# Blocks transposed as float32 in one instruction each, and a group's two sequences kept on the halves of the array

## The chip, the core and the metric

One core of a Trainium2 chip runs the whole program in one launch. The metric is the time of an execution on the device, in microseconds (us). The core has TensorE (PE in the profile; its weight loads are PEld), VectorE (DVE), ScalarE (ACT), GpSimd (POOL) and SyncE (SP), which issues the transfers here. TensorE writes to PSUM alone; the other engines copy from there.

## What is computed

Two layers of a decoder on 1024 tokens of width 1024, all float32. Layer A is gated linear attention with four heads. Layer B, which the change is mostly about, is attention of 8 query heads over three groups of shared keys and values. In group g a query attends keys at distances 0, d, 2d, ..., up to a window:

```python
SWA_GROUPS = ((128, 1), (512, 4), (2048, 16))     # (window, dilation d)
scores = jnp.einsum('brnqgpe,brnkge->brngpqk', qb, kcat)      # per subsequence t = i*d + r
scores = jnp.where(mask, scores, -jnp.inf)
m = jnp.max(scores, axis=-1, keepdims=True)
p = jnp.exp(scores - m)
den = jnp.sum(p, axis=-1)
o = jnp.einsum('brngpqk,brnkge->brnqgpe', p, vcat) / den
lse = m + jnp.log(den)
# over the groups:
wts = jax.nn.softmax(jnp.stack(lses, axis=0), axis=0)
o = jnp.sum(wts[..., None] * jnp.stack(outs, axis=0), axis=0)
y = (o * jax.nn.silu(g)) @ w_out
```

With 1024 tokens the third group (number 2 in the code, dilation 16) has sixteen subsequences of 64 tokens, and its window covers all earlier tokens of the same subsequence.

## The kernel before

The whole program is recorded first, as operations on named tiles; the class `Sched` then sorts them. Its `order()` (line 249) gives each engine its instructions by the earliest time at which they can start in a model of the chip; the durations come from `cost()` (line 521), among them 0.057 us for a two-byte transpose and a rate of 190 KB/us for transfers, to which line 352 adds 2.0 us until they land. Where an operation may run on several engines (`S.va` is VectorE or ScalarE, `S.vap` also GpSimd), the model picks one. The chip gets one fixed order per engine; so every change of a cost re-sorts the whole program. Nearly all instructions are issued from line 441, so the profile's groups are told apart by tile names.

A projection (`project`) multiplies weights by activations in three products of rounded parts (`wh` by `xh`, `wh` by `xl`, `wl` by `xh`; `x1h` and `x1l` in layer B), 512 columns each, into a PSUM tile `acc`. Weights come as 512 KB tiles `wf` and are split into `wh` and `wl` ahead of use.

Layer B has eight units, one per query head (`u`). `q_proj(u)` makes the three `Q`; `scores(u)` multiplies `Q` by the shared keys `K` into tiles `lv`, adds a mask and takes the row's minimum of the negated scores on VectorE (`P<-lv,bmask` or `rmask`), and takes the exponential on ScalarE. The row statistics `sts` go through DRAM (`std`, `nat`, `cwd`, `cw`), since the three groups order their queries differently, and come back as one weight per row. `attend(u)` scales `P` by these weights, transposes its blocks with `turn_blocks` (line 655) into `PT`, and multiplies by the values `V` into `po`. `turn_blocks` also turns layer A's keys (`ke` to `kh`, 8 blocks a head) and, in `rows`, half of the residual stream (`x1f` to `x1r`, 4 blocks for each of 8 tiles).

`turn_blocks` treats a float32 block as two planes of 16 bits, lying interleaved in memory. Each plane is transposed by itself as bfloat16 against `identb`, into a PSUM tile `ms` that keeps the planes apart, and two copies (of `uint16`) put them together again: per block two weight loads and two matmuls, per group of three or four blocks two copies.

Group 2 lies in eight blocks of 128 positions (`BL[2]`, line 1229). A block holds the tokens with the same remainder by 8, which are two subsequences of dilation 16; the 128x128 scores of the two against each other are masked by `rmask`, and their zeros are multiplied by `V` like the rest. A unit has 8, 12 and 15 blocks to turn in groups 2, 1 and 0.

In the profile a float32 product is two records on PE, each with its own weight load; a rounded one (`wh` by `xh`) or a two-byte transpose is one record.

Of the kernel before, what the change touches and what calls it, by code (L numbers as in the profile page):

```python
# [15 lines left out]
T = 1024  # L16
# [123 lines left out]
class Sched:  # L140
# [108 lines left out]
    def order(self):  # L249
# [62 lines left out]
        while n_done < len(ops):  # L312
# [37 lines left out]
            if e == "SP":  # L350
                dma_free = max(dma_free, st) + c
                o.t1 = dma_free + 2.0
                free[e] = st + 0.1
# [167 lines left out]
def cost(e, meth, n, outs, ins, args, kw):  # L521

    if e == "PE":
        if meth == "transpose":
            return 0.057 if ins[0].dtype == BF else 0.215
# [48 lines left out]
def trunk(tc, xT, wP, wA, wAv, wa, w2, b2, ng, wO, wK, wV, wB, wOB, lng, lnb,  # L574
# [80 lines left out]
    def turn_blocks(dst, blocks):  # L655


        n = len(blocks)
        pt = ps.tile([128, 2, 4, 128], BF, name="ms", bufs=2)
        with S.group():  # L660
            for i, b in enumerate(blocks):
                for s in range(2):
                    S.tensor.transpose(pt[:, s, i, :], b[:, s, :], identb)
        to = dst.halves(U16)
        pu = pt.bitcast(U16)
        for s in range(2):
            S.va.copy(to[:, s, :], pu[:, s, :n, :].rearrange("p a b -> p (a b)"))
# [10 lines left out]
    identb = const.tile([128, 128], BF, name="identb")  # L678
# [5 lines left out]
    def load_consts():  # L684
        S.sync.dma_start(ident, ident_d)
        S.vector.tensor_copy(identb, ident)
# [23 lines left out]
    def layer_a(t2, t1, after):  # L710
# [200 lines left out]
        def state_prep(h):  # L911
# [13 lines left out]
            for g in range(2):  # L925
                turn_blocks(kh[:, g * 512:g * 512 + 512],
                            [ke.halves(BF)[:, :, c * 128:c * 128 + 128] for c in range(4 * g, 4 * g + 4)])
# [181 lines left out]
    vd = [dram.tile([T, 256], F32, name=f"vd{i}") for i in range(2)]  # L1109
# [13 lines left out]
    def tok_view(ap, g):  # L1123
        if g == 2:
            return ap.rearrange("p (n a b) -> p n a b", n=4, a=16)
        return ap.rearrange("p (i r) -> p i r", r=DIL[g])

    def layer_b(xs):
        bmask = hp.tile([128, 256], F32, name="bmask", bufs=1)
        S.sync.dma_start(bmask, bmask_d)  # L1130
        rmask = hp.tile([128, 128], F32, name="rmask", bufs=1)
# [29 lines left out]
        def proj_v(g):  # L1161
            stage = {}

            def evac(j, acc):
# [8 lines left out]
                if g == 2:  # L1173

                    S.sync.dma_start(vd[1].rearrange("(a n b) e -> n a b e", a=16, n=8)[j], dst)
                elif j % 4 == 3:
                    h = j // 4 * 512
                    S.sync.dma_start(vd[g - 1][h:h + 512, :].rearrange("(n p) e -> p n e", p=128),
                                      pg.rearrange("p (n e) -> p n e", n=4))
# [381 lines left out]
```

## Time and profile before

| | us |
|---|---|
| median of 3 runs (lowest to highest) | 1208.53 (1208.48 to 1209.45) |
| the profiled execution | 1207.9 |
| its span, first to last instruction | 1206.1 |
| TensorE busy in it | 1185.7 |
| VectorE, ScalarE, GpSimd busy | 754.1, 529.9, 219.6 |

The span is what the trace covers; 1.8 us of the execution lie outside it. Busy times are unions of an engine's instructions. Matmuls overlap, so that a record's own length (219 ns for a two-byte transpose) is longer than the distance to the next one's start; the distance is what it takes of the engine.

### The profile page before, as it was taken

To read this page: it belongs to the slowest core of one execution; us is meant where nothing else is said; L and a number is where in the kernel's file an instruction comes from. 1 tells how busy PE (TensorE), PEld (TensorE's weight loads), DVE (VectorE), ACT (ScalarE), POOL (GpSimd) and SP (SyncE) were. 2 spreads that over 40 slices of the span, in tenths; PEclk is the share of its full clock that TensorE was granted. 3 is DMA by queue.
4 is the path that set the end of the run, shared out by engine and by line. 5 is a ranking of instruction groups with operands and counts; after the bars stand their busy time and mean duration, and the time that the engine had idled before them with its cause. 6 is when DMAs were issued, how large, how long until landed. Compare 5 with 4: busy or idle time off the path is not lost.

```text
span 1206.1 us, 20729 instructions
## 1 busy us (share of the span) xinstructions
PE 1185.7 (98%) x8340; PEld 1017.2 (84%) x8340; DVE 754.1 (63%) x1448; ACT 529.9 (44%) x1070; POOL 219.6 (18%) x145
## 2 busy tenths in 40 slices
PE   9999999999999999999999999999999999999996
PEld 7888978988988887789988888888888888888885
DVE  5482962943967698962255655564656566657468
ACT  5452534433563344422114554545362545456242
POOL 0011101211222122420031213040312130203200
PEclk9999999999999999999999999999999999999999
DMA  8102111111243462554411111111412020124545
GB/s 264 41 20 70 36 54 53 59 49 36 71 165 114 148 211 99 196 184 141 131 56 41 46 37 54 37 53 36 132 46 55 36 55 19 38 63 133 172 133 183
DMA packets 93648, 107.57 MB, mean 89 GB/s; under 512 B 43792, under 2 KB 63248, under 8 KB 93552
## 3 DMA queue, kind: packets, MB, share of 16 engines
q1 hardware_dynamic: 93552, 106.25, 28.3%
q8 instruction: 65, 1.06, 0.4%
q14 instruction: 31, 0.25, 0.1%
HBM read 85.06 MB, written 21.17 MB: 88 GB/s over the span
## 4 chain that ended last, share of the span: by engine, by line
PE 88%; DVE 8%; issue 2%; ACT 1%; DMA 1%; POOL 0%; SPq 0%; DVEq 0%; ACTq 0%; POOLq 0%
PE acc L441 62%; PE po L441 9%; PE lv L441 9%; PE ms L441 4%; PE pro L441 3%; DVE rt L441 2%; DVE X L441 2%; DVE wl L441 1%; DVE oT L441 1%; DVE x1l L441 1%; DMA xf<-in_xT 1%; ACT wh L441 0%; DMA cosT<-in_cos 0%; DVE t L441 0%; DVE sq L441 0%
## 5 line engine op out<-in xcount | busy, mean ns | idle before, releaser
L441 PE MATMUL acc<-x1h,wh 128*128 128x512 f32 x608 | 252.2, 415 | 2.0 <-DVE t L441 1.5
L441 PE MATMUL acc<-x1l,wh 128*128 128x512 f32 x608 | 237.5, 391 | 0.7 <-DVE x1l L441 0.6
L441 PE MATMUL acc<-x1h,wl 128*128 128x512 f32 x608 | 237.5, 391 | 0.0
L441 ACT ACTIVATE wh<-wf 128x1024 fp32r<-128x1024 f32 (+2 forms) x102 | 106.0, 1041 | 253.7 <-PE acc L441 201.6
L441 POOL TENSOR_TENSOR wl<-wf,wh 128x1024 fp32r<-128x1024 f32 x46 | 110.2, 2396 | 549.8 <-ACT wh L441 499.0
L441 PEld LDWEIGHTS acc<-x1h,wl 128*128 128x128 f32 x608 | 114.1, 188 | 24.4
L441 PEld LDWEIGHTS acc<-x1h,wh 128*128 128x128 f32 x608 | 114.5, 188 | 23.3 <-DVE t L441 2.0
L441 PEld LDWEIGHTS acc<-x1l,wh 128*128 128x128 f32 x608 | 114.5, 188 | 22.4 <-DVE x1l L441 1.7
L441 ACT ACTIVATE P<-P,sts 128x128 f32<-128x128 f32 (+1 forms) x192 | 84.9, 444 | 56.3 <-DVE sts L441 54.8
L441 DVE TENSOR_TENSOR wl<-wf,wh 128x1024 fp32r<-128x1024 f32 (+2 forms) x56 | 71.6, 1279 | 56.3 <-ACT wh L441 53.7
L441 DVE TENSOR_TENSOR t<-acc,cosT 128x512 f32<-128x512 f32 x60 | 41.3, 689 | 86.1 <-PE acc L441 79.7
L441 DVE TENSOR_TENSOR t<-acc,sinT 64x512 f32<-64x512 f32 x120 | 82.6, 688 | 2.0 <-ACT R L441 0.4
L441 PE MATMUL acc<-xh,wh 128*128 128x512 f32 x208 | 82.6, 397 | 0.0
L441 PE MATMUL acc<-xh,wl 128*128 128x512 f32 x208 | 81.1, 390 | 0.0
L441 PE MATMUL acc<-xl,wh 128*128 128x512 f32 x208 | 81.0, 389 | 0.0
L441 ACT ACTIVATE PT<-ms 128x512 uint16<-128x512 uint16 (+1 forms) x112 | 67.1, 679 | 30.1 <-PE ms L441 27.0
L441 PE MATMUL lv<-K,Q 128*128 128x256 f32 (+1 forms) x384 | 78.8, 324 | 0.0
L441 PE MATMUL acc<-wh,xh 128*128 128x256 f32 x256 | 75.6, 295 | 0.0
L441 PE MATMUL po<-PT,V 128*128 128x128 f32 (+1 forms) x464 | 73.3, 304 | 0.3 <-DVE PT L441 0.3
L441 DVE CUSTOM_DVE_ANT_0 P<-lv,bmask 128x256 f32<-128x256 f32 (+1 forms) x128 | 47.7, 382 | 40.3 <-PE lv L441 39.5
L441 PE MATMUL acc<-wl,xh 128*128 128x256 f32 x256 | 72.4, 283 | 0.3 <-issue 0.3
L441 PE MATMUL acc<-wh,xl 128*128 128x256 f32 x256 | 72.2, 282 | 0.0
(232 smaller groups left out, 2454.3 us busy)
## 6 DMA issues: line engine op xcount, KB each, us to landing
wf<-in_wB SPq DMA_DIRECT2D x32, 512.0 KB, 3.3
wf<-in_wO SPq DMA_DIRECT2D x16, 512.0 KB, 3.3
wf<-in_wOB SPq DMA_DIRECT2D x16, 512.0 KB, 3.8
wf<-in_wA SPq DMA_DIRECT2D x13, 512.0 KB, 3.2
wf<-in_wK SPq DMA_DIRECT2D x12, 512.0 KB, 3.4
wf<-in_wAv SPq DMA_DIRECT2D x8, 512.0 KB, 3.6
res<-in_xT SPq DMA_DIRECT2D x16, 256.0 KB, 2.7
wf<-in_wV SPq DMA_DIRECT2D x8, 512.0 KB, 3.8
```

What stands on the lines that cost most here:

```text
L441: getattr(handle[o.eng], meth)(*[conv(a) for a in args], **{k: conv(v) for k, v in kw.items()})
```

## The change

1. `turn_blocks` turns a block as float32, one transpose against `ident`, and copies the group once. `identb` goes.
2. Group 2 lies in sixteen blocks of 64 positions. Two subsequences are put on the upper and lower 64 partitions of the score tile: 16 products of 64x64 per unit (`place` gives the column), all in one `lv` tile; masking and exponential work on 128x64. A transpose of 128x128 then holds four subsequences, so 4 blocks a unit are turned in place of 8. The value products take 64 rows of `V` and of the turned block each, on the upper or lower half of the rows, 16 per unit, into two `po` tiles.
3. `V` of group 2 is written to DRAM by value head (`vd3`) and read back in four transfers of 64 partitions for each; the statistics and weights pass through DRAM in halves of 64 partitions (8 transfers for `nat` in place of 4, 4 for `cwd` in place of 2, per unit).
4. The planner's numbers: 0.07 us for any transpose, 0.12 for a product of 64 rows, 280 KB/us for transfers and 1.7 us until they land, 0.37 us of SyncE for an issue.

```diff
             if e == "SP":
                 dma_free = max(dma_free, st) + c
-                o.t1 = dma_free + 2.0
-                free[e] = st + 0.1
+                o.t1 = dma_free + 1.7
+                free[e] = st + 0.37
             else:
                 o.t1 = st + c
                 free[e] = o.t1
...
         if meth == "transpose":
-            return 0.057 if ins[0].dtype == BF else 0.215
+            return 0.07
         n = int(_np.prod(outs[0].shape[1:]))
         fast = "float32r" in str(args[2].dtype)
         if fast:
             return n / 2400 + 0.0135 if n >= 256 else 0.215
         if n >= 128:
             return 4 * n / 2400 + 0.009
+        if args[1].shape[0] == 64:
+            return 0.12
         m = args[1].shape[1]
         return {32: 0.02, 64: 0.05}.get(m, 0.43)
     if e == "SP":
-        return 0.1 + int(_np.prod((outs + ins)[0].shape)) * 4 / 190e3
+        return 0.1 + int(_np.prod((outs + ins)[0].shape)) * 4 / 280e3
...
     def turn_blocks(dst, blocks):
...
         n = len(blocks)
-        pt = ps.tile([128, 2, 4, 128], BF, name="ms", bufs=2)
+        pt = ps.tile([128, 4, 128], F32, name="ms", bufs=2)
         with S.group():
             for i, b in enumerate(blocks):
-                for s in range(2):
-                    S.tensor.transpose(pt[:, s, i, :], b[:, s, :], identb)
-        to = dst.halves(U16)
-        pu = pt.bitcast(U16)
-        for s in range(2):
-            S.va.copy(to[:, s, :], pu[:, s, :n, :].rearrange("p a b -> p (a b)"))
+                S.tensor.transpose(pt[:, i, :], b, ident)
+        S.va.copy(dst, pt[:, :n, :].rearrange("p a b -> p (a b)"))
...
         if g == 2:
-            return pg.rearrange("p (b a n) -> p n a b", b=8, a=16)[:, half * 4:half * 4 + 4]
+            return pg.rearrange("p (e a n) -> p n a e", e=16, a=8)[:, half * 4:half * 4 + 4]
         n = 512 // DIL[g]
         return pg.rearrange("p (r i) -> p i r", r=DIL[g])[:, half * n:half * n + n, :]
 
     def tok_view(ap, g):
         if g == 2:
-            return ap.rearrange("p (n a b) -> p n a b", n=4, a=16)
+            return ap.rearrange("p (n a e) -> p n a e", n=4, a=8)
         return ap.rearrange("p (i r) -> p i r", r=DIL[g])
...
-            src = vd[g - 1][:, c * 128:c * 128 + 128]
             if g == 1:
                 for n in range(2):
                     S.sync.dma_start(
                         V[c][g].rearrange("p (r n e) -> p r n e", r=4, n=2)[:, :, n, :],
-                        src[n * 512:n * 512 + 512, :].rearrange("(p r) e -> p r e", r=4))
+                        vd[n * 512:n * 512 + 512, c * 128:c * 128 + 128].rearrange("(p r) e -> p r e", r=4))
             else:
-                S.sync.dma_start(V[c][g].rearrange("p (b e) -> p b e", b=8),
-                                  src.rearrange("(p b) e -> p b e", b=8))
+
+                src = vd3[c].rearrange("(n a s k j) e -> k s a n (j e)", n=8, a=8, s=2, k=2)
+                for k in range(2):
+                    for s in range(2):
+                        S.sync.dma_start(V[c][g][k * 64:k * 64 + 64, s * 512:s * 512 + 512], src[k, s])
...
-              2: [(b * 128, b * 128, 128) for b in range(8)]}
+              2: [(b * 64, b * 64, 64) for b in range(8)]}
         U = [dict() for _ in range(8)]
+
+
+        def place(b):
+            return b % 4 * 128 + b // 4 * 64
...
             for g in (2, 1, 0):
-                step = 4 if g == 2 else 2
+                step = 8 if g == 2 else 2
                 for j0 in range(0, 8, step):
                     sc = ps.tile([128, 512], F32, name="lv", bufs=2)
                     p = small("P", "a", 13)
                     o = 0
+                    if g == 2:
+                        with S.group():
+                            for j in range(8):
+                                for s in range(2):
+                                    x = s * 512 + j * 64
+                                    o = place(j)
+                                    S.tensor.matmul(sc[s * 64:s * 64 + 64, o:o + 64], Q[g][:, x:x + 64],
+                                                     Kc[g][:, x:x + 64], start=True, stop=True)
                     for j in range(j0, j0 + step):
                         qc, kc, nk = BL[g][j]
                         col = column(g, j)
+                        if g == 2:
+                            o = place(j)
                         P[g, j] = p, o
                         px = p[:, o:o + nk]
-                        S.tensor.matmul(sc[:, o:o + nk], Q[g][:, qc:qc + 128], Kc[g][:, kc:kc + nk],
-                                         start=True, stop=True)
+                        if g < 2:
+                            S.tensor.matmul(sc[:, o:o + nk], Q[g][:, qc:qc + 128], Kc[g][:, kc:kc + nk],
+                                             start=True, stop=True)
...
-                    S.sync.dma_start(nat[:, s, 1, :], dst[1, s].rearrange("(n a b) -> a n b", n=8, a=16))
-            with S.landing(GATHER):
+                    for i in range(2):
+                        S.sync.dma_start(nat[i * 64:i * 64 + 64, s, 1, :],
+                                          dst[1, s].rearrange("(n a i b) -> i a n b", n=8, a=8, i=2)[i])
+            with S.landing(GATHER / 2):
                 for s in range(2):
-                    S.sync.dma_start(nat[:, s, 0, :], dst[0, s].rearrange("(b p) -> p b", p=128))
+                    for i in range(2):
+                        S.sync.dma_start(nat[i * 64:i * 64 + 64, s, 0, :],
+                                          dst[0, s].rearrange("(i b p) -> i p b", i=2, b=8)[i])
...
-                    S.sync.dma_start(cwd[u][g].rearrange("(n a b) -> a n b", n=8, a=16), ew[:, g])
+                    for i in range(2):
+                        S.sync.dma_start(cwd[u][g].rearrange("(n a i b) -> i a n b", n=8, a=8, i=2)[i],
+                                          ew[i * 64:i * 64 + 64, g])
...
-                    bl.append(p.halves(BF)[:, :, o:o + 128])
+                    bl.append(p[:, o:o + 128])
...
-            for hb in range(2):
-                t = turn([(4 * hb + s, 0) for s in range(4)], 2)
-                po = ps.tile([128, 512], F32, name="po", bufs=2)
-                for s in range(4):
-                    S.tensor.matmul(blk(po, s), blk(Vc[2], 4 * hb + s), t[:, s, :], start=True, stop=True)
-                S.vector.tensor_copy(og.rearrange("p (n a b) -> p a n b", n=8, a=16)[:, :, :, 4 * hb:4 * hb + 4],
-                                      po.rearrange("p (b a n) -> p a n b", b=4, a=16))
+
+            p, t = P[2, 0][0], small("PT", "d", 4)
+            turn_blocks(t, [blk(p, i) for i in range(4)])
+            po = [ps.tile([128, 512], F32, name="po", bufs=2) for _ in range(2)]
+            with S.group():
+                for s in range(2):
+                    for j in range(4):
+                        for k in range(2):
+                            h = slice(k * 64, k * 64 + 64)
+                            S.tensor.matmul(po[k][:, s * 256 + j * 64:s * 256 + j * 64 + 64],
+                                             blk(Vc[2], s * 4 + j)[h], t[h, j * 128 + s * 64:j * 128 + s * 64 + 64],
+                                             start=True, stop=True)
+            for k in range(2):
+                for s in range(2):
+                    x = s * 8 + k * 4
+                    S.vector.tensor_copy(
+                        og.rearrange("p (n a e) -> p n a e", n=8, a=8)[:, :, :, x:x + 4],
+                        po[k][:, s * 256:s * 256 + 256].rearrange("p (j a n) -> p n a j", j=4, a=8))
             po = [ps.tile([128, 512], F32, name="po", bufs=2) for _ in range(2)]
```

TensorE, the start of unit 0's `attend` (the rows between are weight loads and passes of the same two tiles, and the six products of a projection), before:

```order
L441 LDWEIGHTS P_6285
L441 MATMUL ms_6661<-identb_201,P_6285 128x128
...
L441 LDWEIGHTS P_6292
L441 MATMUL ms_6674<-identb_201,P_6292 128x128
...
L441 MATMUL acc_6683<-x1h1_4468,wl_6499 128x512
L441 MATMUL po_6700<-PT_6689,V02_6118 128x128 x4
```

and after:

```order
L441 MATMUL ms_6591<-ident_116,P_6218 128x128 x4
L441 MATMUL ms_6600<-ident_116,P_6252 128x128 x3
...
L441 MATMUL acc_6604<-x1h1_4426,wl_6418 128x512
L441 MATMUL po_6620<-PT_6610,V02_5988 128x64
L441 MATMUL po_6621<-PT_6610,V02_5988 128x64
```

Sixteen passes (two groups of four blocks, all of group 2) have become four transposes of group 2 and three of group 1, and the value products alternate between two `po` tiles of 64 columns.

TensorE, the scores of unit 1's group 2 (key tile `K02`), which run within unit 0's `attend`, the first and the third of eight, before:

```order
L441 MATMUL po_6743<-PT_6720,V01_5795 128x128
L441 MATMUL po_6747<-PT_6720,V01_5795 128x128 x2
L441 MATMUL lv_6751<-K02_5040,Q_6647 128x128
L441 LDWEIGHTS P_6359
L441 MATMUL ms_6754<-identb_201,P_6359 128x128
...
L441 MATMUL lv_6800<-K02_5040,Q_6647 128x128
```

and after, with what stands around it:

```order
L441 MATMUL ms_6695<-ident_116,P_6343 128x128 x3
L441 MATMUL ms_6695<-ident_116,P_6351 128x128
L441 MATMUL lv_6702<-K02_5003,Q_6577 64x64 x16
L441 MATMUL po_6671<-PT_6700,V00_4631 128x256
L441 MATMUL po_6671<-PT_6700,V00_4631 128x128
```

The eight products, spread over the attend into two `lv` tiles, have become sixteen in one piece.

ScalarE, the copies of the same `attend`, before:

```order
L441 ACTIVATE wh_6670<-wf_6515 128x1024
L441 ACTIVATE PT_6689<-ms_6661 128x512 x2
L441 ACTIVATE PT_6698<-ms_6674 128x512 x2
L441 ACTIVATE PT_6720<-ms_6706 128x384 x2
L441 ACTIVATE PT_6741<-ms_6726 128x384 x2
```

and after:

```order
L441 ACTIVATE wh_6596<-wf_6434 128x1024
L441 ACTIVATE PT_6610<-ms_6591 128x512
L441 ACTIVATE PT_6617<-ms_6600 128x384
L441 ACTIVATE PT_6649<-ms_6641 128x384
L441 ACTIVATE PT_6654<-ms_6645 128x384
```

Each group's two copies have become one. Over the eight units there are 72 groups in place of 80, and in the whole program TensorE has 54 runs of consecutive transposes in place of 60.

## Rows read from the trace of the kernel before

**Rows 1.** Page: span; each engine's busy us (share of the span) and instructions.
```profile
span 1206.1 us, 20729 instructions
PE 1185.7 (98%) x8340; PEld 1017.2 (84%) x8340; DVE 754.1 (63%) x1448; ACT 529.9 (44%) x1070; POOL 219.6 (18%) x145
```

**Rows 2.** PE waits, whole span: us in total, times, longest; the first and the eighth row.
```profile
PE lv L441 <- DVE X L441: 3.0, 5, 1.6
...
PE ms L441 <- ACT PT L441: 0.3, 1, 0.3
```

**Rows 3.** By stretch: length, PE, PEld, DVE, ACT, POOL busy us (instructions), clock, DMA share, GB/s.
```profile
680.00:1110.00 430.00, 429.34 (x2569) 367.14 (x2567) 260.31 (x710) 216.95 (x592) 94.33 (x72) 1.00 0.21 57
1110.00:1206.00 96.00, 85.76 (x379) 70.49 (x377) 65.53 (x96) 34.76 (x53) 7.58 (x4) 0.97 0.47 154
```

**Rows 4.** PE by form: records, busy us, mean ns of one, idle before.
```profile
L441 PE MATMUL ms<-identb,P 128*128 128x128 bf16 x560 | 39.5, 219 | 0.4 <-ACT PT L441 0.3
```

**Rows 5.** PE in order of time, unit 0's attend: start us, length us, what, how many.
```profile
679.67 1.07 PE L441 MATMUL ms<-identb,P 128*128 128x128 bf16 x16
680.54 0.48 PE L441 MATMUL acc<-x1h,wh 128*128 128x512 f32 x1
680.86 0.39 PE L441 MATMUL acc<-x1l,wh 128*128 128x512 f32 x1
```

**Rows 6.** PE weight loads in the same stretch, same columns.
```profile
679.66 0.90 PEld L441 LDWEIGHTS <-P 128*128 128x128 bf16 x16 [0.26 <-issue]
680.52 0.19 PEld L441 LDWEIGHTS acc<-x1h,wh 128*128 128x128 f32 x1
680.63 0.19 PEld L441 LDWEIGHTS acc<-x1l,wh 128*128 128x128 f32 x1
...
683.31 0.97 PEld L441 LDWEIGHTS po<-PT,V 128*128 128x128 f32 x8
```

**Rows 7.** PE in order of time: 512-column products, then ten 256-column ones, first and last.
```profile
632.36 0.39 PE L441 MATMUL acc<-x1h,wh 128*128 128x512 f32 x1
...
633.49 0.39 PE L441 MATMUL acc<-x1h,wl 128*128 128x512 f32 x1
...
64.72 0.28 PE L441 MATMUL acc<-wh,xl 128*128 128x256 f32 x1
...
65.80 0.28 PE L441 MATMUL acc<-wh,xl 128*128 128x256 f32 x1
```

**Rows 8.** Weight loads by form: records, busy us, mean ns of one, idle before.
```profile
L441 PEld LDWEIGHTS po<-PT,V 128*128 128x128 f32 x464 | 64.6, 191 | 8.3 <-ACT PT L441 4.2 <-DVE PT L441 0.5
L441 PEld LDWEIGHTS <-P 128*128 128x128 bf16 x560 | 34.6, 98 | 5.0 <-issue 2.5 <-ACT P L441 0.8 <-DVE P L441 0.7
L441 PEld LDWEIGHTS lv<-X 128*64 128x64 f32 x64 | 2.2, 137 | 2.5 <-issue 2.2
```

**Rows 9.** PE in order of time: scores of unit 0's group 2 between projections.
```profile
633.72 0.60 PE L441 MATMUL lv<-K,Q 128*128 128x128 f32 x4
...
634.39 0.40 PE L441 MATMUL acc<-x1l,wh 128*128 128x512 f32 x1
```

**Rows 10.** PE around a 64-column product of layer A, then its weight loads.
```profile
222.28 0.28 PE L441 MATMUL acc<-wh,xl 128*128 128x256 f32 x1
222.49 0.69 PE L441 MATMUL lv<-X 128*64 128x64 f32 x16
...
223.33 0.28 PE L441 MATMUL acc<-wl,xh 128*128 128x256 f32 x1
...
222.49 0.55 PEld L441 LDWEIGHTS lv<-X 128*64 128x64 f32 x16
```

**Rows 11.** ScalarE by form: records, busy us, mean ns of one, idle before.
```profile
L441 ACT ACTIVATE PT<-ms 128x512 uint16<-128x512 uint16 x61 | 40.1, 744 | 16.4 <-PE ms L441 15.5 <-DVE PT L441 0.7
...
L441 ACT ACTIVATE th<-acc 128x512 f32<-128x512 f32 x16 | 9.4, 588 | 7.9 <-PE acc L441 7.8
```

**Rows 12.** DMA issues: count, KB each, median us to landing.
```profile
nat<-std SPq DMA_DIRECT2D x32, 4.0 KB, 2.5
```

More of the change, by code (lines that the diff above doesn't have):

```diff
@@ L677, in trunk @@
     lnbc = const.tile([128, 2, NK], F32, name="lnbc")
-    identb = const.tile([128, 128], BF, name="identb")
     epsc = const.tile([128, 1], F32, name="epsc")
@@ L685, in load_consts @@
         S.sync.dma_start(ident, ident_d)
-        S.vector.tensor_copy(identb, ident)
         S.sync.dma_start(ones, ones_d)
@@ L926, in state_prep @@
                 turn_blocks(kh[:, g * 512:g * 512 + 512],
-                            [ke.halves(BF)[:, :, c * 128:c * 128 + 128] for c in range(4 * g, 4 * g + 4)])
+                            [blk(ke, c) for c in range(4 * g, 4 * g + 4)])
             H[h].update(qe=qe, dec=dec, kh=kh, S=None)
@@ L1107, in trunk @@
     kvd = [dram.tile([128, T], F32, name=f"kvd{i}") for i in range(4)]
-    vd = [dram.tile([T, 256], F32, name=f"vd{i}") for i in range(2)]
+    vd = dram.tile([T, 256], F32, name="vd")
+    vd3 = [dram.tile([T, 128], F32, name=f"vd3{c}") for c in range(2)]
     ogB = [dram.tile([128, T], F32, name=f"ogB{k}") for k in range(NK)]
@@ L1130, in layer_b @@
         S.sync.dma_start(bmask, bmask_d)
-        rmask = hp.tile([128, 128], F32, name="rmask", bufs=1)
+        rmask = hp.tile([128, 64], F32, name="rmask", bufs=1)
         S.sync.dma_start(rmask, rmask_d)
@@ L1172, in evac @@
                     S.vector.tensor_copy(dst, acc)
-                if g == 2:
-                    S.sync.dma_start(vd[1].rearrange("(a n b) e -> n a b e", a=16, n=8)[j], dst)
-                elif j % 4 == 3:
+                if j % 4 == 3:
                     h = j // 4 * 512
-                    S.sync.dma_start(vd[g - 1][h:h + 512, :].rearrange("(n p) e -> p n e", p=128),
-                                      pg.rearrange("p (n e) -> p n e", n=4))
+                    rows = pg.rearrange("p (n e) -> p n e", n=4)
+                    if g == 1:
+                        S.sync.dma_start(vd[h:h + 512, :].rearrange("(n p) e -> p n e", p=128), rows)
+                    else:
+                        for c in range(2):
+                            S.sync.dma_start(vd3[c][h:h + 512, :].rearrange("(n p) e -> p n e", p=128),
+                                              rows[:, :, c * 128:c * 128 + 128])
             project_tok(wV[g], xs, [(j, lambda x, j=j: blk(x, j)) for j in range(8)], evac)
@@ L1196, in rows @@
             S.sync.dma_start(f, x1d[et][:, 512:1024])
-            turn_blocks(t, [f.halves(BF)[:, :, i * 128:i * 128 + 128] for i in range(4)])
+            turn_blocks(t, [blk(f, i) for i in range(4)])
             for i in range(4):
@@ L1529, in _arrays @@
     a["bmask"] = np.where((rel >= 0) & (rel <= 128), f4(0), f4(NEG)).astype(f4)
-    q, k = np.meshgrid(r(128), r(128), indexing="ij")
-    tq, tk = (128 * (i % 8) + 8 * (i // 8) for i in (q, k))
-    a["rmask"] = np.where((tq % 16 == tk % 16) & (tk <= tq), f4(0), f4(NEG)).astype(f4)
+    q, k = np.meshgrid(r(128) % 64, r(64), indexing="ij")
+    tq, tk = (128 * (i % 8) + 16 * (i // 8) for i in (q, k))
+    a["rmask"] = np.where(tk <= tq, f4(0), f4(NEG)).astype(f4)
     return a
```

2 lines of the change are left out of this document (1 added, 1 removed).

## The prediction

> **What bounds the kernel now.** I read the page's busy shares first: TensorE is busy 1185.7 of the 1206.1 us span, VectorE 63%, ScalarE 44% [rows 1]. Then the list of TensorE's waits: eleven causes, the largest of 3.0 us in all, and those on the transposes' copies 0.3 us [rows 2]. Then the stretches: between 680 and 1110 us, where the attention of layer B runs, TensorE is busy 429.34 of 430 us at the full granted clock; only the end, after 1110, has some 10 us without it [rows 3]. So the program is one stream of matmuls, and what leaves that stream shortens the span almost one to one, unless a new wait opens. The copies that ScalarE and VectorE save are not on the path.
>
> Since matmuls overlap, I price them by distance from start to start. The timeline merges a run into one row; its length less the mean length of one record, over the count less one, is the distance.
>
> **Transposes, before.** One block costs two two-byte passes. Sixteen passes take 1.07 us, one lasts 0.219 [rows 4, 5]: (1.07 − 0.22)/15 = 0.057; their weight loads give (0.90 − 0.098)/15 = 0.053 [rows 6, 8]. I take 0.056. The code has 8 units of 35 blocks (8, 12 and 15 for the three groups), 32 of layer A's keys and 32 of x1: 344 blocks, 688 passes, 38.5 us. There is also a tail. The next four-byte weight load starts only with the last pass, at 680.52, and the load behind it 0.11 later [rows 6], while the pass has gone after 0.056; the next products run 680.54 and 680.86 where the cadence is 0.227, so the first began in effect at 680.63, 0.06 late [rows 5, 7]. The order of before has 60 such runs: 3.6 us.
>
> **Transposes, after.** Group 2 needs 4 blocks for 8, so 248 + 64 = 312 blocks. Built, the program has 8,220 matmuls for 8,340 [rows 1]; 688 two-byte passes go, the new scores and value products add 256 records (a float32 product is two records here), so each float32 transpose is one record, one load and one stream of 128 columns. No row of before shows one. From below: the two-byte pass, 0.056. From above: the weight load of a 128-column four-byte block, which repeats after (0.97 − 0.19)/7 = 0.111 [rows 6, 8]. Between them lies the price of streaming four-byte data once: 512 columns every 0.227 us (1.13/5), 256 every 0.120 (1.08/9) [rows 7], so 0.107 per 256 columns and 0.0135 on top, which makes 0.067 for 128. I take 0.067, an estimate from those rows, because the transpose is one such pass and the two-byte rows show a transpose going at the pace of its stream: 312 × 0.067 = 20.9 us. The tail shrinks to 0.111 − 0.067 = 0.044 over 54 runs, 2.4 us. Together **−17.6 − 1.2 = −18.8 us** (0.056: −22; 0.111, no tail: −7.5).
>
> The two-byte block loads in 98 ns and the four-byte one in 191 [rows 8]. The Trainium skill, "TensorE: Matmul & The Clock Gate", section "Weight-path perf modes — Fast Weight Load (FWL) and DoubleRow", speaks against the change here: weights load fast only when they are not FP32, and the trace agrees with 98 against 191 ns. The same page, section "Terms", calls transpose mode four times faster for FP32, which no row here shows; a quarter of two records at 0.111 would be 0.056 and the sum 3 us lower.
>
> **Group 2's scores.** Before, 16 records of 128 columns a unit. In unit 0 four of them stand from 633.72 to the second product at 634.39, less one product of 0.227: 0.44 us, 1.77 a unit [rows 7, 9]. After, 16 products of 64×64, 32 records, alternating between two column halves. Layer A has that very form: the last full product at 222.28 (the next due at 222.40), 16 records, and full products again, the second at 223.33, so resumed at 223.21: 0.81 us [rows 10]. Loads there follow each other after (0.55 − 0.137)/15 = 0.028 us [rows 8, 10], so the halves run side by side; 16 more records add 0.45. Thus 1.26 a unit, of which 0.36 is going into and out of the divided array. 8 × (1.26 − 1.77) = **−4.1 us**.
>
> That 0.36 us is what the Trainium skill, "TensorEngine Tiling (Array Packing)", section "Key Properties", leads one to expect: changing the tiling mode drains TensorE; the trace agrees.
>
> **Group 2's value products.** Before, 16 records at 0.111: 1.78 us a unit [rows 6]. After, 32 records, each with 64 rows and a full 128-column load, alternating between the two row halves, and streams of only 64 columns, so the loads set the pace. No row shows row halves. If both load side by side, as the column halves do, 16 pairs × 0.111 + 0.36 = 2.14 a unit, **+2.9 us** in all; if one after the other, 32 × 0.111 + 0.36 = 3.91, +17.0. I take the first, the nearest form being the column halves [rows 10].
>
> **What else moves.** One copy of 128×512 per group in place of two of 0.744 us [rows 11]; a plain float32 copy of that size is nearest to 0.588 [rows 11]. It makes the planner place the value products closer to their transposes. In unit 0 of before 1.30 us lies between the end of the transposes (680.74) and their first use (682.04) [rows 5]. Priced with the distances above, 12 of the 72 places in the changed order have under 1.2 us of TensorE's work between, down to 0.9. Draining (0.22 − 0.06) plus a copy of 0.5 to 0.6 plus two hand-overs needs about 0.9. I put **+1 us** there, 0 to 5. Six more small transfers a unit queue on SyncE, behind waits on the statistics; each lands in about 2.5 us [rows 12], and the attend waits for them only under the next unit's projections, so nothing, or 1 to 2 us in unit 7, where these are fewest. The table of transfers only re-sorts loads that TensorE hardly waits for: ±2 us. The `identb` cast, smaller masks and longer runs of V lie beside TensorE.
>
> **Sum.** −18.8 − 4.1 + 2.9 + 1 = −19.0 us. The profiled execution took 1207.9 us, 1.8 outside its span, and 0.6 below the median of 1208.53. 1207.9 − 19.0 = 1188.9; against the median, **1189.5 us**.
>
> **The rivals.** First, the transposes go at the pace of their loads: 0.111 us a block, two passes' price for one. For it: four-byte loads never come closer than that [rows 6]; against it: in the two-byte transposes the stream sets the pace [rows 5, 6]. Transposes give −7.5 in place of −18.8: 1200.8 us. This is what the Trainium skill's rule on fast loads, above, would make of it, since the new blocks are FP32; its chance is this rival's.
>
> Second, the row halves load in turn: +17.0 in place of +2.9, 1203.6 us. For it: no row shows them apart; against it: the column halves do overlap.
>
> Third, on the other side: TensorE streams float32 transposes in four passes, as it does a float32 product, which needs two records of 0.111 for 128 columns. 312 × 0.222 = 69.3 us, no tail: +27.2 for the transposes, and with −4.1 + 2.9 + 1 this gives 1235.5 us. It turns the change into a loss once a block costs over 0.136 us (38.5 + 3.6 + 0.2 over 312). Against it: one record per block, not two.
>
> Fourth, the copies come late after all: if every one of the 72 groups made TensorE wait 0.15 us, +11 us, 1199 us.
>
> **How the numbers follow.** Forecast 0.60 (1184 to 1195, from 0.056 a block with no new wait to 5 us of waits); loads set the pace 0.18; row halves in turn 0.09; four passes 0.07; late copies 0.06. Under 0.2% (2.4 us) a measurement of this kernel hardly tells from no change. All but four passes end faster, less some share for two of them falling together (−7.5 with +17.0: 1214.9, slower): faster 0.89, same 0.03, slower 0.08. The range, 1184 to 1204, takes in the forecast, late copies, nearly all of the load-bound case and half of the row halves.
>
> **What would show it.** Transposes in the changed timeline: runs of four with about 0.067 us from start to start (0.111 says loads, 0.2 four passes). Value products of group 2 in pairs every 0.11 us. Between 680 us and the end of the attention TensorE still busy over 99%, without waits on the copies `PT` of over a few us in all, and its record count at 8,220. I am wrong if its busy time doesn't fall by some 18 us, or falls while its waits grow.

## The result, and the profile after

| | before | after |
|---|---|---|
| median of 4 runs each, us (lowest to highest) | 1208.99 (1208.48 to 1209.57) | 1195.51 (1194.38 to 1196.20) |
| the profiled execution | 1207.9 | 1194.93 |
| its span | 1206.1 | 1193.1 |
| TensorE busy | 1185.7 | 1173.8 |

The ratio is 0.9887, with an interval of 0.987 to 0.9905: the kernel is 13.5 us (1.1%) faster. The forecast was 1189.5, so some 30% of the expected gain is missing, and it will turn out that what is left comes in good part from other terms than those it was put on.

The page of after, span and engines (it answers to [rows 1]): TensorE is still the bound, and its records are the 8,220 that were counted ahead.

```profile
span 1193.1 us, 20435 instructions
PE 1173.8 (98%) x8220; PEld 1006.7 (84%) x8220; DVE 760.7 (64%) x1448; ACT 477.4 (40%) x1000; POOL 191.9 (16%) x126
```

Busy time by stretch, after (as [rows 3]; stretch, its length, then busy us and instructions of each engine, granted clock, share of the DMA engines, GB/s). Between 680 and 1110 TensorE doesn't pause, at the full clock; so the matmuls show no new wait there.

```profile
680.00:1110.00 430.00, 429.99 (x2552) 365.42 (x2551) 271.27 (x726) 181.60 (x547) 72.36 (x54) 1.00 0.21 59
1110.00:1194.00 84.00, 75.05 (x331) 61.76 (x330) 59.23 (x84) 28.39 (x41) 1.29 (x1) 0.97 0.49 166
```

TensorE in order of time, after, in three stretches (as [rows 5, 7]): start us, length us, what, how many.

```profile
753.27 1.04 PE L441 MATMUL ms<-ident,P 128*128 128x128 f32 x8
754.23 1.15 PE L441 MATMUL lv<-K,Q 128*64 128x64 f32 x32
...
683.31 2.00 PE L441 MATMUL po<-PT,V 64*128 64x64 f32 x32
685.25 0.88 PE L441 MATMUL ms<-ident,P 128*128 128x128 f32 x6
...
1184.66 0.39 PE L441 MATMUL acc<-woh,ogl 128*128 128x512 f32 x1
```

Weight loads in order of time, after: around the same value products (as [rows 6]).

```profile
683.31 1.86 PEld L441 LDWEIGHTS po<-PT,V 64*128 64x128 f32 x32 [0.36 <-ACT PT L441]
685.24 0.64 PEld L441 LDWEIGHTS ms<-ident,P 128*128 128x128 f32 x6
685.85 0.19 PEld L441 LDWEIGHTS acc<-x1h,wh 128*128 128x128 f32 x1
685.96 0.19 PEld L441 LDWEIGHTS acc<-x1l,wh 128*128 128x128 f32 x1
```

Transposes and their weight loads by form, after (as [rows 4, 8]): records, busy us, mean ns of one, idle before.

```profile
L441 PE MATMUL ms<-ident,P 128*128 128x128 f32 x248 | 34.4, 274 | 0.0
L441 PEld LDWEIGHTS po<-PT,V 128*128 128x128 f32 x336 | 45.4, 191 | 3.9 <-ACT PT L441 1.1
L441 PEld LDWEIGHTS ms<-ident,P 128*128 128x128 f32 x248 | 28.9, 140 | 4.3 <-ACT PT L441 0.2
```

A float32 transpose repeats every (1.04 − 0.274)/7 = **0.109 us**. The forecast had 0.067; the two passes of before took 2 × 0.056 = 0.112. So the block costs TensorE what it cost before.

The value products come as 16 pairs: their loads repeat every (1.86 − 0.188)/15 = 0.111 us for two, so the row halves load side by side, as forecast. The 0.36 us ahead of the first load is put down to the copy `PT`, but ScalarE had done that copy at 682.58, while the load in front ended at 682.95; the same 0.36 to 0.37 stands in all eight units and belongs to the way into the halves. The scores' 16 pairs take (1.15 − 0.222)/15 = 0.062 on average with the first interval, which holds the change of mode; as forecast.

Marks in both traces show where the 13.0 us of the span went (start of the named matmul, after less before): the second column sum of layer A's second normalization 475.92 for 474.94, +1.0; the first transposes of unit 0 681.06 for 679.67 [rows 5], +1.4; those of unit 7 1084.90 for 1093.66, −8.8; the last matmul 1184.66 for 1195.37, −10.7; the end −13.0. So layer A lost about 2 us between two column sums (what follows behind them is told under the table, below), the seven units from 0 to 7 gained 10.2 (1.45 each), unit 7 and the last projection 2.0, and the work behind the last matmul 2.3.

### The profile page after: what moved, and what is told of

Same layout as the page of the kernel before. It is cut to its first block, busy times and chain, and to the rows that moved or that the text cites. A ratio compares the mean times of both kernels' runs of the same rounds, so it can differ in the third digit from the quotient of the medians.

```text
span 1193.1 us, 20435 instructions
## 1 busy us (share of the span) xinstructions
PE 1173.8 (98%) x8220; PEld 1006.7 (84%) x8220; DVE 760.7 (64%) x1448; ACT 477.4 (40%) x1000; POOL 191.9 (16%) x126
## 4 chain that ended last, share of the span: by engine, by line
PE 92%; DVE 5%; issue 1%; ACT 1%; DMA 1%; SPq 0%; POOL 0%; DVEq 0%; ACTq 0%; POOLq 0%
PE acc L441 66%; PE po L441 10%; PE lv L441 9%; PE ms L441 4%; PE pro L441 3%; DVE X L441 2%; DVE t L441 1%; DVE oT L441 1%; DMA xf<-in_xT 1%; DVE rt L441 0%; DVE K L441 0%; ACT wh L441 0%; DVE b L441 0%; DVE sum L441 0%; DVE x1l L441 0%
## 5 line engine op out<-in xcount | busy, mean ns | idle before, releaser
L441 DVE TENSOR_TENSOR wl<-wf,wh 128x1024 fp32r<-128x1024 f32 (+2 forms) x57 | 74.2, 1301 | 64.7 <-ACT wh L441 64.3
L441 ACT ACTIVATE P<-P,sts 128x128 f32<-128x128 f32 (+2 forms) x192 | 81.2, 425 | 45.1 <-DVE sts L441 44.2
L441 DVE TENSOR_TENSOR Q<-t,t 128x512 f32<-128x512 f32 x48 | 71.4, 1488 | 1.6
L441 PE MATMUL lv<-K,Q 128*64 128x64 f32 (+2 forms) x512 | 68.3, 286 | 0.0
L441 PE MATMUL po<-PT,V 64*128 64x64 f32 (+2 forms) x592 | 68.2, 293 | 0.0
```

The source lines that it names most:

```text
L441: getattr(handle[o.eng], meth)(*[conv(a) for a in args], **{k: conv(v) for k, v in kw.items()})
```

## The experiments

Theory A, formed after the result: a float32 block is bound by its stream, at 0.109; the gain left comes from the tails (0.06 us behind each of 60 runs of transposes, now about 0.01: in the rows above the load behind the transposes at 685.85 is followed by the next one after 0.11, just when the last pass is done), from group 2's halves, and from fewer loads that wait for copies. Rival L: the load sets the pace (the prediction's first rival). Rival R: the copies are worth nothing, and what the priced terms leave over came from a lucky order.

**e1: the float32 transposes alone**, in the kernel before (with the single copy and the price of 0.07; halves and table as before).

```diff
-                for s in range(2):
-                    S.tensor.transpose(pt[:, s, i, :], b[:, s, :], identb)
+                S.tensor.transpose(pt[:, i, :], b, ident)
...
-        for s in range(2):
-            S.va.copy(to[:, s, :], pu[:, s, :n, :].rearrange("p a b -> p (a b)"))
+        S.va.copy(dst, pt[:, :n, :].rearrange("p a b -> p (a b)"))
```

> The kernel before with the float32 transposes and the single copy alone; group 2 and the transfers' table stay. Theory A (the changed trace: a float32 block costs 0.109 us because its stream of 128 columns takes that long, and the single copy frees TensorE's weight loads from waiting for PT): 344 blocks x 0.109 = 37.5 us against 688 x 0.056 = 38.5, so -1.0; no tail after 60 runs, -3.3; some 3.8 us of late loads go to 2.0, -3.8: about -8 us, 1201. Rival R (the gain over the priced terms came from a lucky order): -1.0 - 3.3 = -4.3 us, 1204.5.

Measured 1201.18, ratio 0.9931 (0.9919 to 0.9944): 7.4 us faster. In that kernel 344 blocks at 0.109 save 1.0 us of stream and the tails some 3; the other 3 are left for waits, which e1 alone doesn't show. Theory A's number holds here.

**e2: the halves of group 2 alone**, with two-byte transposes and the old table.

> The kernel before with group 2's halves alone: two-byte transposes with two copies, the transfers' table of before. Both theories: 624 two-byte passes for 688, -3.6; scores 8 x (1.28 - 1.77) = -3.9; value products 8 x (2.09 - 1.78) = +2.5: -5.0 us, 1204. Theory A: nothing more, as the copies stay double. Rival R: the extra gain of 3 to 4 us may fall here as well, 1200.

Measured 1206.2, 0.9977 (0.9967 to 0.9986): 2.4 us faster, short of the expected 5. From the first transposes of unit 0 to those of unit 4 it gains 4.0 us, 1.0 a unit, more than the 0.63 that the terms make; but from unit 6 to the last matmul it gives nearly 6 us back. TensorE's waits over 1 us that before doesn't have (what waited, who for, us in all, times, longest) lie in that stretch, two of the three on the split halves `ogh` and `ogl` of the attention's result. Behind the waits at 1093 and 1099 us the granted clock also falls to 0.50, for 3.41 us from 1100.11.

```profile
PE acc L441 <- DVE ogl L441: 1.9, 3, 1.5
...
PE ms L441 <- ACT PT L441: 1.9, 2, 1.1
PE acc L441 <- ACT ogh L441: 1.4, 1, 1.4
```

**e3: the table of transfers alone**, in the kernel before.

```diff
-                o.t1 = dma_free + 2.0
-                free[e] = st + 0.1
+                o.t1 = dma_free + 1.7
+                free[e] = st + 0.37
...
-        return 0.1 + int(_np.prod((outs + ins)[0].shape)) * 4 / 190e3
+        return 0.1 + int(_np.prod((outs + ins)[0].shape)) * 4 / 280e3
```

> The kernel before with the transfers' table alone (1.7, 0.37, 280). Theory A: TensorE hardly waits for transfers, so 0 within 2 us, 1207 to 1211. Rival T (the table sorts the ends better: the last 8.1 us behind the matmuls in place of 10.4): -2 to -3 us, 1206. If the table caused the longer waits at the end of layer A (4.0 us at 473 to 477 in place of 1.6): +2 us.

Measured 1206.67, 0.9985 (0.9974 to 0.9995), about 2 us faster: between the two theories. Two places stand out in the marks, +1.8 in layer A's second normalization and −2.8 behind the last matmul.

**e4: the kernel after with the old table** (e3's edit taken back).

> The changed kernel with the transfers' table of before. Theory A: the same as the changed kernel within 2 us, 1194 to 1198, with TensorE's attention from the first transpose to the last value product in 420 us as in the changed kernel. Rival T: slower by the 2 to 3 us that the table gave, about 1198.

Measured 1201.55, 0.9933 (0.992 to 0.9945). Theory A's "no difference" was wrong: without the new table the kernel is 6 us slower. Up to unit 6 it runs even with after or ahead of it; the loss comes behind that, with waits like those of e2. The profiled execution, 1199.07, is the fastest of five, with a mean clock of 0.998; the other four took 1200.97 to 1201.94 at 0.995 to 0.997, so a part of the 6 us is a lower clock.

```profile
PE acc L441 <- ACT ogh L441: 2.1, 1, 2.1
...
PE po L441 <- ACT PT L441: 1.1, 1, 1.1
```

**e5: half the stream under the same load.** In the kernel after, the 64 blocks of `ke` and `x1f` are turned in two halves of 64 rows, side by side: each load has still 128 columns, each stream only 64.

```diff
-                S.tensor.transpose(pt[:, i, :], b, ident)
+                for k in range(2):
+                    h = slice(k * 64, k * 64 + 64)
+                    S.tensor.transpose(pt[k][:, i, :], b[h], ident[h, h])
```

> The changed kernel, but the 64 blocks of layer A's keys and of x1 are turned in two halves of 64 rows, on the two row halves of the array, against the matching quarter of the identity: per half a load of 128 columns and a stream of 64. Theory A (the stream sets the pace, 0.109 us for 128 columns; the float32 transpose's load takes 0.058): two halves side by side cost max(0.058, 0.055), about 0.06 us a block within a run. Rival L (the load of a 128-column float32 block sets the pace, as in the prediction's first rival): 0.11 us a block, as for the value products on row halves. The whole kernel may be slower, since each run of transposes now divides the array.

Loads and matmuls of one group of four blocks, four pairs, in e5:

```profile
506.90 0.32 PEld L441 LDWEIGHTS ms<-ident,x1f 64*128 64x128 f32 x8 [0.35 <-issue]
...
506.90 0.46 PE L441 MATMUL ms<-ident,x1f 64*128 64x64 f32 x8
```

The pairs' loads follow each other after (0.32 − 0.139)/3 = 0.060 us. A load of float32 for a transpose thus takes no more than 0.060, and with half the stream the pace is nearly halved: the stream sets it, and rival L falls. That the load had only 64 rows is not the reason: nine times in after, a float32 load for a transpose with all 128 rows begins 0.058 to 0.061 behind the one before it, where 0.109 is usual. (The run's time, 1199.26 in a single execution, also holds the changes of mode and the second copy of each group, and tells nothing of this.)

**e6: every group copied twice**, in the kernel after (`for _ in range(2):` ahead of the copy).

> The changed kernel, but each group is copied out of PSUM twice, the second copy over the first, and the planner counts both. TensorE's own work is that of the changed kernel. Theory A (the single copy is worth some 3.8 us because TensorE's loads no longer wait for PT): +2 to +4 us against the changed kernel, 1198 to 1200, with more idle time of the weight loads that PT ends. Rival R: the copies lie beside TensorE and cost nothing, within 1 us of the changed kernel, 1195 to 1196.5.

Measured 1194.83, 0.9886 (0.9872 to 0.99): no slower than after. ScalarE is busy 511.7 us for 477.4, and TensorE doesn't feel it. That theory A lives on fewer copies is wrong, and R is right in this: their number is worth nothing, with a planner that counts them.

**e7: the kernel after with two-byte transposes** (e1's edit taken back, all else kept).

> The changed kernel with the two-byte transposes and two copies of before; group 2's halves and the transfers' table stay. Theory A: 624 x 0.056 = 34.9 us against 312 x 0.109 = 34.0, +0.9; tails of 0.055 after 54 runs, +3.0; late loads, +3.8: +7.7 us, 1203. Rival R: +3.9 us, 1199.5. The forecast's price of 0.067 us a block would have made this +14 us, 1209.

Measured 1203.54, 0.9957 (0.9944 to 0.9969): 8.0 us over after. The float32 form is worth 7 to 8 us in both surroundings (e1, e7), though its stream is worth only 1 us; R's number is 3 to 4 us off in both. But in e7 the rest isn't late loads. The loads of the turned blocks wait for VectorE's `og` there, and for no copy `PT`:

```profile
L441 PEld LDWEIGHTS po<-PT,V 128*128 128x128 f32 x336 | 47.7, 191 | 5.4 <-DVE og L441 1.3
```

By the marks of the two profiled executions e7's span is 10.0 us longer than that of after: 3.4 of it ahead of unit 0 (1.2 in the first 15 us, before any block is turned; stream and tails make some 0.9), 2.9 in the seven units, of which stream and tails make some 2.5, and 3.7 behind the first transposes of unit 7. What the rest comes from, other than another order and another execution, isn't shown; so theory A had the number of e7 right, and its term for late loads not.

**e8: the kernel after with the measured price** (0.109 for 0.07 in the planner).

> The changed kernel with 0.109 us for a transpose in the planner in place of 0.07, the measured distance. Theory A: the same work in an order that fits it better by a little, 0 to -2 us, 1193.5 to 1195.5. Rival: any new order costs or gives 1 to 2 us by chance, so between 1193.5 and 1197.5.

Measured 1196.54, 0.99 (0.9887 to 0.9913), no better than after; the wrong price of the transposes did no harm that can be told.

**e9: the kernel before with the measured price of its copies.** e1 and e6 left some 3 us that go with the float32 form but not with the number of copies. The planner had 580 ns for a two-byte copy of 128×512 on ScalarE, which takes 744 [rows 11]; so it placed value products before their copies were done.

```diff
         if outs[0].dtype == U16:
-            c += 0.09
+            c += 0.25
...
         if outs[0].dtype == U16:
-            c += 0.04
+            c += 0.12
```

> The kernel before, with one edit in the planner's price of a two-byte copy: 0.09 becomes 0.25 on the scalar engine and 0.04 becomes 0.12 on the vector engine, which is what the profiled copies take (128x512: 744 and 733 ns against the 580 and 643 ns that the planner had). Nothing of the work changes. Theory P (the late loads in attention, worked out as 5.8 us in the kernel before and nearly gone once the blocks are float32, came from copies that the planner thought shorter than they are): the loads that wait for copies go, 1208.6 - 3 = 1205.5, and the idle time ahead of the loads of the turned blocks falls from 8.3 to under 5 us. Theory C (they come from the blocks' two streams or from something else that the price doesn't touch): within 1 us of 1208.6, the idle time stays near 8.

Measured 1205.51, 0.9976 (0.9966 to 0.9985), 3.0 us faster, without any change of the work. The loads of the turned blocks by form, in e9, e1 and after (the row of before is the first of [rows 8], idle 8.3):

```profile
L441 PEld LDWEIGHTS po<-PT,V 128*128 128x128 f32 x464 | 64.8, 191 | 4.0
```

```profile
L441 PEld LDWEIGHTS po<-PT,V 128*128 128x128 f32 x464 | 62.3, 191 | 3.7 <-ACT PT L441 0.2
```

The wait for ScalarE's copies (4.2 of the 8.3) is gone in both; after, with 336 such loads, has 3.9 and waits 1.1. Theory P holds for the order of before: its late loads were the planner's error of 0.09 to 0.16 us on each of a group's two copies. The float32 form has one copy a group, of 0.58 us where the planner has 0.49 (its row stands below, under e10); e1's row shows the waits gone with it. The same error doesn't cost this in every order: e2 and e7 keep the two copies and their price, and `PT` ends 0.4 us and none of this idle time. By the marks 1.7 of e9's 2.6 us of span lie between the first transposes of unit 0 and of unit 7; ahead of unit 0 it loses 0.9, and behind that of unit 7 it gains 1.8, which re-sorting alone may have done.

**e10 to e12: which number of the table.** The kernel after, with the table's three numbers apart. e10 has only the issue of 0.37 us, e11 only the rate and the latency, e12 only the rate.

```diff
-                o.t1 = dma_free + 1.7
-                free[e] = st + 0.37
+                o.t1 = dma_free + 2.0
+                free[e] = st + 0.1
...
         return 0.1 + int(_np.prod((outs + ins)[0].shape)) * 4 / 280e3
```

(This is e12's.)

> The kernel after, with the transfers' table half way back: the issue of a transfer still costs SyncE 0.37, but the latency is 2.0 and the rate 190e3 again. Theory I (the issue time is what keeps unit 7 of attention and the tail free of waits, the latency and the rate are what moved layer A's second normalization to be 1.9 us later): unit 7 as in the kernel after, the stretch from the fifth to the seventh column sum back to 17.8, together 1195.5 - 1.9 = 1193.6. Theory J (latency and rate keep unit 7 free): like the old table, 1201.5.

> The kernel after, with the other half of the table back: latency 1.7 and rate 280e3 stay, the issue costs SyncE 0.1 again. Theory I: waits in unit 7 as with the old table and layer A still 1.9 late, so 1201.5 to 1203. Theory J: 1195.5 or 2 less, with unit 7 free of waits.

> The kernel after, of whose three numbers in the transfers' table only the rate is left (280e3); latency 2.0 and issue 0.1 as in the kernel before. Theory K (the rate alone frees unit 7 and the tail, and the latency alone moves layer A's second normalization): unit 7 free of waits, the stretch from the fifth to the seventh column sum 17.8 again, so 1.5 to 2 under the run with both: 1192.3. Theory M (the rate does both): within 1 of the run with both, 1194.1, stretch 19.6. Theory N (the latency frees unit 7): like the old table, 1201.5, stretch 17.8.

| | us | ratio | layer A, sixth to eighth product of the column sums |
|---|---|---|---|
| after (all three) | 1195.51 | 0.9887 (0.987 to 0.9905) | 19.6 us |
| e10, issue | 1201.49 | 0.9934 (0.9922 to 0.9946) | 17.8 |
| e11, rate and latency | 1194.11 | 0.988 (0.9864 to 0.9895) | 19.6 |
| e12, rate | 1194.58 | 0.9882 (0.9866 to 0.9899) | 19.6 |
| e4, none | 1201.55 | 0.9933 (0.992 to 0.9945) | 17.8 |

The last column goes from start to start in the profiled execution; the expectations, which count from zero, call it the fifth to the seventh column sum. The rate alone does everything, the loss in layer A included; theory I was wrong, J and then M hold. Where the 6 us go can be seen on ScalarE in order of time. First e10, then e12, in unit 7's attend (in brackets the idle time ahead of an instruction and who ended it):

```profile
1085.52 0.58 ACT L441 ACTIVATE PT<-ms 128x512 f32<-128x512 f32 x1
1086.00 0.62 ACT L441 ACTIVATE ogh<-ogf 128x512 fp32r<-128x512 f32 x1
1090.44 0.63 ACT L441 ACTIVATE ogh<-ogf 128x512 fp32r<-128x512 f32 x1 [3.82 <-DMA ogf<-ogB]
1092.22 2.00 ACT L441 ACTIVATE ogh<-ogf 128x512 fp32r<-128x512 f32 x3 [1.15 <-DMA ogf<-ogB]
```

```profile
1085.88 0.62 ACT L441 ACTIVATE ogh<-ogf 128x512 fp32r<-128x512 f32 x1
1086.78 1.37 ACT L441 ACTIVATE ogh<-ogf 128x512 fp32r<-128x512 f32 x2 [0.28 <-DMA ogf<-ogB]
```

and on TensorE in e10 the product that needs it:

```profile
1092.90 0.51 PE L441 MATMUL acc<-ogh,wh 128*128 128x512 f32 x1 [1.80 <-ACT ogh L441]
```

With the old rate ScalarE sits 3.8 us in front of a transfer of the attention's result (`ogf` from `ogB`, 256 KB), and the output projection waits for its half `ogh`; with the new rate the order has no such wait. Behind that product e10 also runs at the lower clock for 3.41 us (stretch, length, busy us and instructions of each engine, granted clock, share of the DMA engines, GB/s), and products of 512 columns follow each other after 0.43 us in place of 0.23:

```profile
1094.26:1097.67 3.41, 3.41 (x10) 2.67 (x9) 3.41 (x8) 3.41 (x10) 0.00 (x0) 0.50 0.02 1
```

That the order has no such wait is not because the new rate is nearer to the truth: in before such a transfer took 5.1 us from issue to landing (page, DMA issues: count, KB each, median us to landing), where the old table says 1.48 + 2.0 and the new one 1.04 + 1.7.

```profile
ogf<-ogB SPq DMA_DIRECT2D x12, 256.0 KB, 5.1
```

Why the order that falls out of 280 KB/us suits this end better isn't settled; latency and issue time weren't tried without it together. e11 and e12 lie 1 us under after, within the intervals; neither is a better version that can be told from it.

## Why the prediction was partly right

**The bound: right.** What left the stream of matmuls shortened the span: TensorE is busy 11.9 us less and the span is 13.0 shorter. The busy time should have fallen by some 18, which was named as the sign of an error. (Some 2 us of what is missing there went into a stretch at the lower clock, below.)

**Transposes: the step that failed.** "I take 0.067 [...] because the transpose is one such pass." It was worked out from rounded products, 512 columns at 0.227 us [rows 7], and the argument for it was one record for one block. One record is not one pass: it takes 0.109, and its record is 274 ns long where a two-byte one is 219 [rows 4], longer by about one two-byte pass of 0.056. The rows that were nearer in kind, the plain float32 products, which stream 128 columns in 2 × 0.111, were used for the bound of the third rival only. Stream and tails: 38.5 + 3.6 us before; 312 × 0.109 = 34.0 and about 0.3 after. That is −7.8, not −18.8, and of it −3.6 is owed to the 32 blocks that group 2 no longer has to turn, −0.9 to the price of a block (0.109 for 0.112) and −3.3 to the tails.

The upper bound that the prediction gave, 0.111 without a tail and −7.5, was right in size and wrong in its reason: the load, its supposed cause, takes at most 0.060 (e5). The Trainium skill, "TensorE: Matmul & The Clock Gate", section "Weight-path perf modes — Fast Weight Load (FWL) and DoubleRow", rules out fast loads for FP32; plain float32 blocks agree (191 ns), the float32 blocks that are transposed don't (140 ns, and 0.060 apart in e5), and here the measurement decides. The same page's factor of four for FP32 in transpose mode (section "Terms") isn't seen either, if it is meant against a float32 product: 0.109 against 0.222 for one of 128 columns is a factor of two.

**Group 2's scores and value products: right.** Worked out from all their places in the trace, with what it takes to enter and leave the halves, 1.28 us a unit for the scores (1.26 forecast; −3.9) and 2.09 for the value products (2.14; +2.5). Rival 2, halves in turn, is out by the pairs at 0.111. e2, with the two-byte blocks, gains 6.1 us through six units, where the terms make 3.8; so their gain is there, with something on top.

**Late copies: wrong sign.** +1 was put there; about 3 us went the other way. The view that could have shown it is the first of [rows 8]: 4.2 us of idle time ahead of the value products' loads, ended by ScalarE's copy `PT`. The prediction read only the matmuls' waits, where it was 0.3 us [rows 2], and took the loads for covered. e9 shows the cause in the kernel before; that the order with the halves has few of these waits with either form of transpose (e2, e7) was not foreseen either.

**The table: not a side matter.** ±2 was given because "TensorE hardly waits for" the loads. Its net effect in the kernel before is −1.9 (e3), inside that; in the changed kernel it decides over 6 us (e4), since the new order without it runs into the waits for `ogh` and, in e10, into a lower clock behind them. In after it costs 1.8 in layer A, where TensorE now waits for the column sums (after, in order of time),

```profile
473.47 0.49 PE L441 MATMUL ms<-sum,onesr 128*128 128x512 f32 x1 [1.44 <-ACT sum L441]
475.92 0.80 PE L441 MATMUL ms<-sum,onesr 128*128 128x512 f32 x1 [1.96 <-DVE sum L441]
477.35 0.79 PE L441 MATMUL acc<-x1h,wh 128*128 128x512 f32 x1 [0.63 <-DVE t L441]
...
482.81 0.39 PE L441 MATMUL acc<-x1h,wl 128*128 128x512 f32 x1
```

and another 2.2 us right behind them, which no theory above had: from 475.17 to 482.00 the granted clock is 0.50, the lower of its two levels (1.2 and 2.4 GHz). In before it stays at 1.00 (stretch, length, busy us and instructions of each engine, clock, DMA; after, then before):

```profile
475.17:482.00 6.83, 5.45 (x12) 3.98 (x13) 6.49 (x10) 1.78 (x3) 0.15 (x1) 0.50 0.20 77
```

```profile
475.17:482.00 6.83, 6.45 (x28) 5.13 (x28) 6.25 (x10) 2.88 (x5) 0.00 (x0) 1.00 0.26 90
```

The same fifteen products of the projection, from the first behind the sums, take 482.81 − 477.35 = 5.46 us from first to last start in after and 479.13 − 475.82 = 3.31 in before:

```profile
475.82 0.50 PE L441 MATMUL acc<-x1h,wh 128*128 128x512 f32 x1 [0.38 <-DVE t L441]
...
479.13 0.39 PE L441 MATMUL acc<-x1h,wl 128*128 128x512 f32 x1
```

Every profile with the rate of 280 has this stretch in layer A (e3, e5 to e8 and e12 6.83 us, e11 3.41), and of those with 190 only e1 (3.41). At 505 us before waits 1.1 us for `x1h` and `x1l`, which after, being late, doesn't; so at unit 0 the mark stands only 0.4 higher than at the sum.

At the end the table gives about 2.3. There the chain of waits of before runs through a backlog of VectorE (start us, us, what), while in after VectorE is waiting for TensorE's last product:

```profile
1184.88 5.01 PE po L441 x23
1189.89 2.59 DVE rt L441 x4
...
1198.76 1.41 DVE rt L441 x2
```

```profile
1179.61 5.45 PE acc L441 x24
1185.07 0.02 issue
1185.09 0.70 DVE rt L441
```

From the last matmul's start to the end it is 10.75 us before and 8.48 after; with the old table it is 9.7 to 10.8 (before, e1, e2, e4, e10), with the new one 7.9 to 8.6 (after, e3, e5 to e8, e11, e12). e9, at 9.5 with the old table, shows that another order moves this end by itself too.

**The sum as measured**: transposes and tails −7.8, scores −3.9, value products +2.5, late loads about −3 (in the seven units the three terms before make −7.4 of the −10.2), the waits for the column sums +1.8, the lower clock +2.2, the waits for `x1h` and `x1l` −1.1, the end −2.3: −11.6 of −13.0. What the other 1.4 us are stays open. That the measured time still lies only 6 us from the forecast and inside its range is in part luck: the transposes missed their term by 11 us, and late loads and the end, which had not been forecast with that sign, gave some 6 us back, while the waits and the lower clock in layer A took 4. No wait on the statistics' added transfers stands among TensorE's waits after. The first rival, with the block's price nearly right, gave 1200.8; what it lacks to 1195.5 is in the main the late loads and the end. Its chance of 0.18 was too small, since no row spoke for 0.067 but those of rounded products.

## What to carry to other kernels

One instruction in the profile isn't one pass: price a float32 transpose by a float32 row, not by a rounded product. Where a planner sorts the instructions, compare its price of every copy with the profiled one, and read the idle time ahead of the weight loads by form as well as the matmuls' waits, since a late copy shows there first. A wait of TensorE can cost more than its length, so the granted clock behind it is read too. A number of a planner is part of the kernel: a change should be tried with the planner's numbers before and after, because the order that goes well with the one may not go well with the other.

## What the runs showed of the hardware

- A float32 transpose of 128×128 is one record, one weight load and 0.109 us; two two-byte transposes take 2 × 0.056. The stream sets its pace (e5).
- Its weight load lasts 140 ns and repeats in no more than 0.060 us (e5), where the plain float32 load of the same 128 columns lasts 191 ns and repeats after 0.111.
- Products on the two row halves, 64 rows with a load of 128 columns each, load side by side: a pair every 0.111 us. Transposes on them run at a pair in 0.060.
- Going from the whole array to halves and back costs at both ends: against the pace of the runs on either side, about 0.1 us on the way in and 0.2 on the way out, for the column halves of the scores as for the row halves of the value products.
- The granted clock fell to 0.50 for 6.83 us in after, behind a wait of TensorE of 1.44 us and within one of 1.96, and for 3.41 us in e10 behind waits of 1.15 and 1.80; in e4's profiled execution it stayed at 1.00 behind waits of 1.1 and 2.1. At 0.50 a 512-column product takes 0.43 us in place of 0.23.
